# A decoder trunk's prologue rewritten: loads, conditioning row and row scale

## Chip, cores and metric

One core of a Trainium2 chip runs the whole kernel. The metric is device time in microseconds (us) of one execution; lower is better. The engines are TensorE (PE in the rows, PEld where it loads weights), VectorE (DVE), ScalarE (ACT), GpSimd (POOL) and SyncE (SP), which issues the loads.

## What is computed

One layer on 256 tokens of 1024 channels, in float32. Cut to the part that matters here:

```python
shift, scale, gate = jnp.split(c @ w_ada[l] + b_ada[l], 3, axis=-1)
h = rmsnorm(x, norm_pre[l]) * (1.0 + scale[:, None]) + shift[:, None]
proj = h @ w_in[l] + b_in[l]
...
out = merged @ w_out[l]
x = x + gate[:, None] * rmsnorm(out, norm_post[l])
```

`rmsnorm` divides each token's row by the root of its mean square plus 1e-6. Between `proj` and `merged` lie three token mixers, which the change does not touch.

## The kernel before

Python code issues the instructions of all engines in one order, written out by `trunk`; a class `Loom` estimates when each instruction ends and weaves side work between the matrix products. Each engine executes its own instructions strictly in that order. Almost every instruction goes through one helper line, L158, so the rows tell instructions apart by their tiles.

**Prologue (L295 to L460).** TensorE first multiplies a tile of ones with itself (`heat`, L299; `HEAT = (9, 8, 12)` gives the number of products at the three places), so that its clock rises. SP loads the first half of x (128 tokens, `x_sb[:, 0]`), the row c, the second half of x and a few parameters (`p_sb`), in this order (L311 to L314). VectorE clears `c_sb` first (L308), because c fills one row of a 128-row tile, and SP's load of c waits for that. Two products with ones put c into every partition (`ps_cb`, L322); ScalarE copies them to `cb`.

For each half t of the tokens (L441): the sum of squares (ScalarE for t = 0, VectorE for t = 1), then `rsqrt` (L420: reciprocal on VectorE, root on ScalarE, and three small VectorE operations that refine it), then ScalarE multiplies the rows by the result, and eight TensorE transposes (`flip`, tile `ps_x`) turn channels into partitions. A run of `heat` products follows each half. `evac_x` copies the transposed blocks to `xn`: first those of channels 0 to 511 (`evac_x(0, ...)` on ScalarE), the others on VectorE inside the first step of the next loop (L489).

**Wave stage (L475).** Eight steps k, one for each 128 channels. Each loads 1 MB of `w_ada` (`a_raw`) and 1 MB of input weights (`w_raw`); VectorE forms two dot products of `a_raw` with `cb` (`ada_dot`) and from them the columns `acol` and `bcol`; ScalarE splits the weights (`w_hi`) and makes `h_hi` and `h_f` from `xn`, `acol` and `bcol`; VectorE subtracts for the low parts `w_lo` and `h_lo`; TensorE then has 48 products (tile `w`), half of them with the first weight tile, half with the second:

```python
act.copy(hi[0], wraw[:, 0])
if k < CATCH:
    act.copy(hi[1], wraw[:, 1])
act.activation(h_hi[:, k], xn[:, k], AF.Identity, scale=a, bias=b)
act.activation(h, xn[:, k], AF.Identity, scale=a, bias=b)
...
dve.tensor_tensor(lo[0], wraw[:, 0], hi[0], op=OP.subtract)
dve.tensor_tensor(h_lo[:, k], h, h_hi[:, k], op=OP.subtract)
dve.tensor_tensor(lo[1], wraw[:, 1], hi[1], op=OP.subtract)
```

The VectorE dots of step k + 1 stand behind the last of these lines.

**Tail (L1309).** For each half of the tokens two output banks (`ps_out`) are squared on ScalarE with row sums, multiplied by the gate row on VectorE (`weigh`), and after the inverse root multiplied and added to x (`finish`), which also stores them.

Of the kernel before, what the change touches and what calls it, by code (L numbers as in the profile page):

```python
# [18 lines left out]
D = 1024  # L19
# [32 lines left out]

CATCH = 7
AHEAD = {2: ((0, 1), (2,), (3,), ()), 0: ((0,), (1,), (2,), (3,))}
HEAT = (9, 8, 12)
LEAD = 2
BANKS = dict(mm=3, sd=3, ml=2)
BIG, MID = 10, 3
# [6 lines left out]


class Loom:
    """Issues the instructions of every engine in the order of the trace and estimates when each one ends, so that
    side work can be woven between the matrix products once its operands are due."""

    HOP = {"pe": 250.0, "act": 130.0, "dve": 150.0, "dma": 0.0}
    OWN = {"pe": 0.0, "act": 140.0, "dve": 125.0, "dma": 0.0}
# [25 lines left out]
    def drop(self, *tiles):  # L98
        for t in tiles:
            for ring in self.rings.values():  # L100
                if t.tensor.name in ring["live"]:
                    ring["live"].remove(t.tensor.name)
                    ring["free"].append(self.last.get(t.tensor.name, 0.0))
# [37 lines left out]
        return end  # L141

    def clocked(self, start, cost):
        """The tensor engine runs at half its clock after a window in which it was mostly idle."""
        w = int(start // 3413)
        while self.window < w:
            self.cold = self.busy < (0.9 if self.cold else 0.5) * 3413
            self.busy = 0.0
            self.window += 1
        self.busy += cost * (2 if self.cold else 1)  # L150
        return cost * (2 if self.cold else 1)
# [64 lines left out]
                self.tasks.remove(task)  # L216

    def spawn(self, gen, rank=2):
        """Ranks: 0 for what the tensor engine needs next, 1 for the chains of the heads, 2 for the rest."""
        task = [0.0, gen, False, rank]  # L220
        i = next((i for i, t in enumerate(self.tasks) if t[3] > rank or (t[3] == rank == 1)), len(self.tasks))
        self.tasks.insert(i, task)
        return task
# [34 lines left out]
def trunk(ctx: ExitStack, tc, xtok, crow, wada, wave0, wgrp, wmisc, w1, wbr, wout, par, vbias, out):  # L258
# [30 lines left out]
    def mm(o, l, r, start, stop, **kw):  # L289
        return pe.matmul(o, l, r, start=start, stop=stop, **kw)  # L290
# [3 lines left out]

    ones = const.tile([128, 128], F32, name="ones")  # L295
    pool.memset(ones, 1.0)
    warm = const.tile([128, 1], F32, name="warm")

    def heat(n):  # L299
        ps = bank("ps_heat")  # L300
        for _ in range(n):
            mm(ps[:, 0:128], ones, ones, True, True)
        drop(ps)

    heat(HEAT[0])
    act.activation(warm, ones[:, 0:1], AF.Sqrt)
    c_sb = midt("c_sb", [128, D])
    dve.memset(c_sb, 0.0)  # L308
    x_sb = bigt("x_sb", shape=[128, 2, D])
    p_sb = const.tile([128, NPAR], F32, name="p_sb")  # L310
    loom.load(nc.sync, x_sb[:, 0], xtok[:, 0:D])  # L311
    loom.load(nc.sync, c_sb[0:1, :], crow)
    loom.load(nc.sync, x_sb[:, 1], xtok[:, D:2 * D])
    loom.load(nc.sync, p_sb[:, 0:NEARLY], par[:, 0:NEARLY])  # L314

    def pc(name, i=0, n=1):
        return p_sb[:, PAR[name] + i:PAR[name] + i + n]
# [3 lines left out]
    cb = const.tile([128, D], F32, name="cb")  # L321
    ps_cb = [bank("ps_cb", "sd") for _ in range(2)]  # L322
    for i in range(2):
        mm(ps_cb[i], ones, c_sb[:, 512 * i:512 * i + 512], True, True)

    def causal(o, rows_ge_cols, fill):
        pool.affine_select(out=o, in_=o, compare_op=OP.is_ge, fill=fill, base=0,
# [100 lines left out]
    def at_once(gen):  # L428
        for _ in gen:
            pass  # L430
# [5 lines left out]
    def evac_x(i, copy):  # L436
        for t in range(2):
            copy(xn[:, 4 * i:4 * i + 4, 128 * t:128 * t + 128], ptr[t][i].rearrange("p (k q) -> p k q", k=4))
            drop(ptr[t][i])

    for t in range(2):  # L441
        ss, r, n = [work.tile([128, 1], F32, name=f"x{n}{t}", bufs=1) for n in "srn"]
        if t == 0:
            act.activation(xnf[:, 0:D], x_sb[:, 0], AF.Square, accum_out=ss)
        else:
            dve.scalar_tensor_tensor(xnf[:, D:2 * D], x_sb[:, 1], 1.0, x_sb[:, 1], op0=OP.mult, op1=OP.mult,
                                     accum_out=ss)
        dve.tensor_scalar(ss, ss, 1.0 / D, 1e-6, op0=OP.mult, op1=OP.add)
        at_once(rsqrt(ss, r, n))
        for i in range(2):  # L450
            c = x_sb[:, t, 512 * i:512 * i + 512]
            act.activation(c, c, AF.Copy, scale=r)
            for k in range(4):
                flip(ptr[t][i][:, 128 * k:128 * k + 128], c[:, 128 * k:128 * k + 128])
        if t == 0:
            for i in range(2):
                act.copy(cb[:, 512 * i:512 * i + 512], ps_cb[i])
                drop(ps_cb[i])
        heat(HEAT[1 + t])
    evac_x(0, act.copy)  # L460

    adac = const.tile([128, 24], F32, name="adac")

# [11 lines left out]
    for k in range(KT):  # L475
# [833 lines left out]
    for t in range(2):  # L1309
        for fs in (range(tail, KT - 1), range(KT - 1, KT)) if t == 0 else (range(tail, KT),):  # L1310
            for c in range(2):
                for f in fs:
                    out_mm(t, c, f)
        r, v, n = [work.tile([128, 1], F32, name=f"o{x}", tag=f"o{x}") for x in "rvn"]
        ss = [work.tile([128, 1], F32, name=f"ss{c}", tag=f"ss{c}") for c in range(2)]
        rs.append(r)
        res.append(midt("res", [128, 2, 512]))
        for c in range(2):
            scr = work.tile([128, 512], F32, name="sqo", tag="p_t")
            act.activation(scr, po[t][c], AF.Square, accum_out=ss[c])  # L1320
        weigh(t, 0)
        dve.tensor_scalar(ss[0], ss[0], D * 1e-6, None, op0=OP.add)
        if t == 0:
            weigh(t, 1)
        else:
            finish(0, 1)
        dve.tensor_scalar(v, ss[0], ss[1], 1.0 / D, op0=OP.add, op1=OP.mult)
        dve.reciprocal(r, v)
        act.activation(r, r, AF.Sqrt)
        if t == 1:  # L1330
            weigh(t, 1)
        dve.tensor_scalar(n, v, r, r, op0=OP.mult, op1=OP.mult)
        dve.scalar_tensor_tensor(r, n, -3.0, r, op0=OP.add, op1=OP.mult)
        finish(t, 0)
# [89 lines left out]
```

## Time and profile before

| | us |
|---|---|
| median of 3 runs | 512.8 |
| the runs | 513.61, 512.29, 512.80 |
| span of the profiled execution (first to last instruction) | 510.6 |
| TensorE busy in that span | 502.0 (98%) |
| VectorE busy | 431.5 (85%) |
| ScalarE busy | 316.9 (62%) |

Of the profiled execution the span is given, not the time around it; the median of the runs is 2.2 us above that span. A row of the timeline has the start in us from the span's start, the time from the start of its first instruction to the end of its last, engine, line, operation, output<-inputs, shape and count; in brackets, the idle time before and what ended it. Matmul records overlap, so the step from one to the next is shorter than the time of one.

### The profile page before, as it was taken

To read this page: it belongs to the slowest core of one execution; us is meant where nothing else is said; L and a number is where in the kernel's file an instruction comes from. 1 tells how busy PE (TensorE), PEld (TensorE's weight loads), DVE (VectorE), ACT (ScalarE), POOL (GpSimd) and SP (SyncE) were. 2 spreads that over 40 slices of the span, in tenths; PEclk is the share of its full clock that TensorE was granted. 3 is DMA by queue.
4 is the path that set the end of the run, shared out by engine and by line. 5 is a ranking of instruction groups with operands and counts; after the bars stand their busy time and mean duration, and the time that the engine had idled before them with its cause. 6 is when DMAs were issued, how large, how long until landed. Compare 5 with 4: busy or idle time off the path is not lost.

```text
span 510.6 us, 10012 instructions
## 1 busy us (share of the span) xinstructions
PE 502.0 (98%) x3962; PEld 476.6 (93%) x3962; DVE 431.5 (85%) x894; ACT 316.9 (62%) x542; POOL 7.5 (1%) x42
## 2 busy tenths in 40 slices
PE   8999999999999999999999999999999999999994
PEld 6999999899889989979999989999999999999983
DVE  4998888899987998988989968999899997667755
ACT  5556666244566867779568995665534466975442
POOL 4000000000000000000000000000000000000000
PEclk9999999999999999999999999999999999999999
DMA  7999975884694424422523415544675664445502
GB/s 263 380 367 367 421 236 189 292 323 167 223 358 163 164 83 166 143 105 90 190 119 134 162 60 210 197 166 171 243 282 213 235 254 172 166 166 198 214 1 82
DMA packets 17617, 103.86 MB, mean 203 GB/s; under 512 B 2081, under 2 KB 2209, under 8 KB 7458
## 3 DMA queue, kind: packets, MB, share of 16 engines
q1 hardware_dynamic: 17570, 103.22, 55.0%
q8 instruction: 31, 0.51, 0.4%
q14 instruction: 16, 0.13, 0.1%
HBM read 102.16 MB, written 1.05 MB: 202 GB/s over the span
## 4 chain that ended last, share of the span: by engine, by line
PE 96%; DMA 1%; DVE 1%; ACT 0%; issue 0%; DVEq 0%; SPq 0%; ACTq 0%
PE ps_f L158 50%; PE ps_br L158 14%; PE w L158 9%; PE ps_t L158 7%; PE ps_out L158 4%; PE ps_o L158 3%; PE ps_s L158 2%; PE ps_c L158 2%; PE ps_p L158 1%; DMA x_sb<-in_xtok_dram 1%; PE ps_n L158 1%; PE ps_qk L158 1%; PE ps_heat L158 1%; PE ps_g L158 0%; PE ps_ht L158 0%; PE ps_mb L158 0%
## 5 line engine op out<-in xcount | busy, mean ns | idle before, releaser
L158 DVE TENSOR_TENSOR w_lo<-w_raw,w_hi 128x1024 fp32r<-128x1024 f32 x148 | 180.3, 1221 | 34.5 <-ACT w_hi L158 34.2
L158 ACT CAST w_hi<-w_raw 128x1024 fp32r<-128x1024 f32 x148 | 154.1, 1043 | 57.1 <-PE ps_br L158 16.9
L158 PE MATMUL ps_f<-h_hi,w_hi 128*128 128x256 f32 x704 | 177.4, 288 | 0.0
L158 PE MATMUL ps_f<-h_lo,w_hi 128*128 128x256 f32 x704 | 173.5, 283 | 0.0
L158 PEld LDWEIGHTS ps_f<-h_hi,w_hi 128*128 128x128 f32 x704 | 134.8, 192 | 2.2 <-issue 1.9
L158 PEld LDWEIGHTS ps_f<-h_lo,w_hi 128*128 128x128 f32 x704 | 134.9, 192 | 0.6 <-issue 0.2
L158 PE MATMUL ps_f<-h_hi,w_lo 128*128 128x256 f32 x704 | 102.7, 287 | 0.0
L158 DVE SCALAR_TENSOR_TENSOR acc<-u,p_sb,acc 128x226 f32<-128x226 f32 (+28 forms) x232 | 94.5, 463 | 8.6 <-ACT acc L158 8.4
L158 PEld LDWEIGHTS ps_f<-h_hi,w_lo 128*128 128x128 f32 x704 | 91.5, 192 | 2.4 <-issue 2.3
L158 ACT ACT_TABLE_LOAD x27 | 34.6, 1283 | 1.3 <-PEq L1416 0.8
L158 PE MATMUL w<-h_lo,w_hi 128*128 128x256 f32 x128 | 31.4, 283 | 0.0
L158 PE MATMUL w<-h_hi,w_lo 128*128 128x256 f32 x128 | 31.4, 283 | 0.0
L158 PE MATMUL ps_t<-w_hi,h_hi 128*128 128x256 f32 x96 | 29.6, 308 | 0.0
L158 DVE SCALAR_TENSOR_TENSOR a_raw<-a_raw,cb 128x1024 f32<-128x1024 f32 x24 | 28.5, 1220 | 0.0
L158 PE MATMUL ps_t<-w_hi,h_lo 128*128 128x256 f32 x96 | 27.1, 283 | 0.0
L158 PE MATMUL ps_t<-w_lo,h_hi 128*128 128x256 f32 x96 | 27.1, 282 | 0.0
L158 PEld LDWEIGHTS w<-h_hi,w_lo 128*128 128x128 f32 x128 | 24.6, 192 | 0.0
L158 PEld LDWEIGHTS w<-h_lo,w_hi 128*128 128x128 f32 x128 | 24.6, 192 | 0.0
L158 ACT ACTIVATE gs<-ps_f,p_sb 128x256 f32<-128x256 f32 x16 | 7.6, 476 | 25.5 <-PE ps_f L158 22.7
L158 PEld LDWEIGHTS ps_t<-w_hi,h_hi 128*128 128x128 f32 x96 | 18.3, 191 | 2.0 <-issue 1.7
L158 ACT ACTIVATE pm<-pm,mx 128x16 f32<-128x16 f32 (+2 forms) x48 | 19.1, 403 | 0.8 <-DVE mx L158 0.8
L158 PEld LDWEIGHTS ps_t<-w_lo,h_hi 128*128 128x128 f32 x96 | 18.3, 191 | 0.7 <-issue 0.5
(268 smaller groups left out, 777.0 us busy)
## 6 DMA issues: line engine op xcount, KB each, us to landing
w_raw<-in_wgrp_dram SPq DMA_DIRECT2D x50, 1024.0 KB, 4.9
w_raw<-in_wbr_dram SPq DMA_DIRECT2D x12, 1024.0 KB, 4.8
a_raw<-in_wada_dram SPq DMA_DIRECT2D x16, 512.0 KB, 7.3
w_raw<-in_wave_dram SPq DMA_DIRECT2D x16, 512.0 KB, 7.3
w_raw<-in_w_dram SPq DMA_DIRECT2D x8, 1024.0 KB, 4.9
a_raw<-in_wada_dram SPq DMA_DIRECT2D x4, 1024.0 KB, 5.2
w_raw<-in_wout_dram SPq DMA_DIRECT2D x4, 1024.0 KB, 4.9
x_sb<-in_xtok_dram SPq DMA_DIRECT2D x2, 512.0 KB, 4.7
```

What stands on the lines that cost most here:

```text
L158: inst = self.pin(fn(*args, **kw))
```

## The change

- c goes to ScalarE's load queue, and the parameters behind it; both halves of x stand alone at the head of SP's queue. The clearing of `c_sb` is gone: the products that spread c use one row of ones and one row of c. VectorE, not ScalarE, copies them to `cb`, at the head of its order.
- The row scale is no longer multiplied into x. It is put on the diagonal of a 128x128 tile (`diag`, VectorE), and eight float32 products of x with that tile transpose and scale at once; they take the place of the transposes.
- Both sums of squares are on ScalarE, and the root is taken straight from them (a tile `eps` holds 1e-6); VectorE then inverts and refines once.
- `HEAT` is (9, 6, 6).
- In step k = 0 of the wave stage ScalarE copies the other blocks of `xn` behind `h_f`, and the second weight tile's `w_hi` behind them; VectorE's copies of `xn` are gone.
- The tail takes the root straight from the sums too, and the order of `weigh` and the small operations on VectorE changes.

```diff
-HEAT = (9, 8, 12)
+HEAT = (9, 6, 6)
...
+    loom.load(nc.scalar, c_sb[0:1, :], crow)
+    for t in range(2):
+        loom.load(nc.sync, x_sb[:, t], xtok[:, D * t:D * t + D])
+    loom.load(nc.scalar, p_sb[:, 0:NEARLY], par[:, 0:NEARLY])
     heat(HEAT[0])
     act.activation(warm, ones[:, 0:1], AF.Sqrt)
-    dve.memset(c_sb, 0.0)
-    loom.load(nc.sync, x_sb[:, 0], xtok[:, 0:D])
-    loom.load(nc.sync, c_sb[0:1, :], crow)
-    loom.load(nc.sync, x_sb[:, 1], xtok[:, D:2 * D])
-    loom.load(nc.sync, p_sb[:, 0:NEARLY], par[:, 0:NEARLY])
...
-        mm(ps_cb[i], ones, c_sb[:, 512 * i:512 * i + 512], True, True)
+        mm(ps_cb[i], ones[0:1, :], c_sb[0:1, 512 * i:512 * i + 512], True, True)
+        dve.tensor_copy(cb[:, 512 * i:512 * i + 512], ps_cb[i])
+        drop(ps_cb[i])
...
+        act.activation(xnf[:, D * t:D * t + D], x_sb[:, t], AF.Square, accum_out=ss)
+        act.activation(r, ss, AF.Sqrt, bias=eps, scale=1.0 / D)
...
+        dve.tensor_scalar(v, ss, 1.0 / D, 1e-6, op0=OP.mult, op1=OP.add)
+        dve.reciprocal(r, r)
+        dve.tensor_scalar(n, v, r, r, op0=OP.mult, op1=OP.mult)
+        dve.scalar_tensor_tensor(r, n, -3.0, r, op0=OP.add, op1=OP.mult)
+        dve.tensor_scalar(diag, ident, r, -0.5, op0=OP.mult, op1=OP.mult)
         for i in range(2):
-            c = x_sb[:, t, 512 * i:512 * i + 512]
-            act.activation(c, c, AF.Copy, scale=r)
             for k in range(4):
-                flip(ptr[t][i][:, 128 * k:128 * k + 128], c[:, 128 * k:128 * k + 128])
+                mm(ptr[t][i][:, 128 * k:128 * k + 128], x_sb[:, t, 512 * i + 128 * k:512 * i + 128 * k + 128], diag,
+                   True, True)
         heat(HEAT[1 + t])
...
-        if k == 0:
-            evac_x(1, dve.tensor_copy)
...
-        if k < CATCH:
+        if 0 < k < CATCH:
             act.copy(hi[1], wraw[:, 1])
         act.activation(h_hi[:, k], xn[:, k], AF.Identity, scale=a, bias=b)
         act.activation(h, xn[:, k], AF.Identity, scale=a, bias=b)
-        if k >= CATCH:
+        if k == 0:
+            for t in range(2):
+                evac_x(t, 1)
+        if k == 0 or k >= CATCH:
             act.copy(hi[1], wraw[:, 1])
...
+        act.activation(r, ss[1], AF.Sqrt, bias=ss[0], scale=1.0 / D)
...
-        dve.reciprocal(r, v)
-        act.activation(r, r, AF.Sqrt)
...
+        dve.reciprocal(r, r)
```

In the built programs the orders of the engines differ in the prologue, in the first step of the wave stage and in the tail, and nowhere between. VectorE in the prologue, before (`xs` are the sums of squares, `xr` and `xn_...` the scale and its refinement, `a_raw,adac` the first dots):

```order
L158 SCALAR_TENSOR_TENSOR xn,xs_184<-x_sb 128x1024
L158 TENSOR_SCALAR xs_184<-xs_184 128x1
L158 RECIPROCAL xr_185<-xs_184 128x1
L158 TENSOR_TENSOR xn_186<-xr_185,xs_184 128x1
L158 SCALAR_TENSOR_TENSOR xn_186<-xn_186,xr_185 128x1
L158 SCALAR_TENSOR_TENSOR xr_185<-xn_186,xr_185 128x1
L158 SCALAR_TENSOR_TENSOR a_raw,adac<-a_raw,cb 128x1024 x2
```

VectorE at the same place in the changed program:

```order
L158 COPY cb<-ps_cb 128x512 x2
L158 TENSOR_SCALAR xv_159<-xs_156 128x1
L158 RECIPROCAL xr_157<-xr_157 128x1
L158 TENSOR_SCALAR xn_158<-xv_159,xr_157 128x1
L158 SCALAR_TENSOR_TENSOR xr_157<-xn_158,xr_157 128x1
L158 TENSOR_SCALAR diag_168<-ident,xr_157 128x128
L158 TENSOR_SCALAR xv_165<-xs_162 128x1
L158 RECIPROCAL xr_163<-xr_163 128x1
L158 TENSOR_SCALAR xn_164<-xv_165,xr_163 128x1
L158 SCALAR_TENSOR_TENSOR xr_163<-xn_164,xr_163 128x1
L158 TENSOR_SCALAR diag_189<-ident,xr_163 128x128
L158 SCALAR_TENSOR_TENSOR a_raw,adac<-a_raw,cb 128x1024 x2
```

The copies of `ps_cb` now stand ahead of both scale chains. TensorE from its start to the first product of the wave stage, before:

```order
L158 MATMUL ps_heat<-ones 128x128 x9
L158 MATMUL ps_cb<-c_sb,ones 128x512 x2
L158 MATMUL ps_x<-ident,x_sb 128x128 x8
L158 MATMUL ps_heat<-ones 128x128 x8
L158 MATMUL ps_x<-ident,x_sb 128x128 x8
L158 MATMUL ps_heat<-ones 128x128 x12
L158 MATMUL w_0_225<-h_hi,w_hi 128x256 x2
```

TensorE, changed:

```order
L158 MATMUL ps_heat<-ones 128x128 x9
L158 MATMUL ps_cb<-c_sb,ones 128x512 x2
L158 MATMUL ps_x<-diag_168,x_sb 128x128 x8
L158 MATMUL ps_heat<-ones 128x128 x6
L158 MATMUL ps_x<-diag_189,x_sb 128x128 x8
L158 MATMUL ps_heat<-ones 128x128 x6
L158 MATMUL w_0_218<-h_hi,w_hi 128x256 x2
```

The places are the same; transposes became products, and there are eight `heat` products fewer. ScalarE from the first copy of `xn` to the `h_hi` of step k = 1, before:

```order
L158 COPY xn<-ps_x 128x4x128 x2
L158 CAST w_hi<-w_raw 128x1024 x2
L158 ACTIVATE h_hi<-xn,bcol,acol 128x256
L158 ACTIVATE h_f<-xn,bcol,acol 128x256
L158 CAST w_hi<-w_raw 128x1024 x2
L158 ACTIVATE h_hi<-xn,bcol,acol 128x256
```

ScalarE, changed:

```order
L158 COPY xn<-ps_x 128x4x128 x2
L158 CAST w_hi<-w_raw 128x1024
L158 ACTIVATE h_hi<-xn,bcol,acol 128x256
L158 ACTIVATE h_f<-xn,bcol,acol 128x256
L158 COPY xn<-ps_x 128x4x128 x2
L158 CAST w_hi<-w_raw 128x1024 x3
L158 ACTIVATE h_hi<-xn,bcol,acol 128x256
```

The second `w_hi` of step 0 moved from ahead of `h_hi` to behind two more copies.

## Rows read from the trace of the kernel before

**Rows 1.** The page's chain that ended last, shares by engine.
```profile
PE 96%; DMA 1%; DVE 1%; ACT 0%; issue 0%; DVEq 0%; SPq 0%; ACTq 0%
```
**Rows 2.** That chain in order of time: start us, us, what.
```profile
1.08 0.92 DVE c_sb L158
...
2.38 5.78 DMA x_sb<-in_xtok_dram
...
12.70 2.68 PE ps_heat L158 x24
15.39 46.33 PE w L158 x384
```
**Rows 3.** All that TensorE waited for: us in total, times, longest.
```profile
PE ps_heat L158 <- POOL ones L296: 1.1, 1, 1.1
PE ps_x L158 <- ACT x_sb L158: 0.7, 1, 0.7
```
**Rows 4.** Timeline of SP's queue: the first load.
```profile
0.80 0.38 SPq L187 DMA_DIRECT2D x_sb<-in_xtok_dram  x1
```
**Rows 5.** TensorE in the prologue: two tile views (ns min/median/max), two timeline rows.
```profile
L158 PE MATMUL ps_heat<-ones x17: 421/421/582, 1.1 to 4.6; 128*128 128x128 f32 x17
L158 PE MATMUL ps_heat<-ones x16: 275/275/275, 8.8 to 10.4; 128*128 128x128 f32 x16
5.06 2.97 PE L158 MATMUL ps_cb<-c_sb,ones 128*128 128x512 f32 x4
7.86 1.05 PE L158 MATMUL ps_x<-ident,x_sb 128*128 128x128 f32 x8
```
**Rows 6.** Timeline of VectorE, 9.4 to 20 us.
```profile
9.45 0.15 DVE L158 TENSOR_SCALAR xs<-xs 128x1 f32<-128x1 f32 x1
9.64 0.16 DVE L158 RECIPROCAL xr<-xs 128x1 f32<-128x1 f32 x1
...
10.53 1.22 DVE L158 SCALAR_TENSOR_TENSOR a_raw<-a_raw,cb 128x1024 f32<-128x1024 f32 x1
...
13.09 1.28 DVE L158 COPY xn<-ps_x 128x512 f32<-128x512 f32 x2
...
16.20 1.22 DVE L158 TENSOR_TENSOR w_lo<-w_raw,w_hi 128x1024 fp32r<-128x1024 f32 x1
17.34 1.22 DVE L158 SCALAR_TENSOR_TENSOR a_raw<-a_raw,cb 128x1024 f32<-128x1024 f32 x1
...
19.82 0.16 DVE L158 TENSOR_TENSOR acol<-acol,p_sb 128x1 f32<-128x1 f32 x1
```
**Rows 7.** Timeline of ScalarE, 11.9 to 20.6 us.
```profile
11.89 1.05 ACT L158 COPY xn<-ps_x 128x512 f32<-128x512 f32 x2
12.84 2.00 ACT L158 CAST w_hi<-w_raw 128x1024 fp32r<-128x1024 f32 x2
14.73 0.60 ACT L158 ACTIVATE h_hi<-xn,bcol,acol 128x256 fp32r<-128x256 f32 x1
15.23 0.59 ACT L158 ACTIVATE h_f<-xn,bcol,acol 128x256 f32<-128x256 f32 x1
...
20.02 0.60 ACT L158 ACTIVATE h_hi<-xn,bcol,acol 128x256 fp32r<-128x256 f32 x1
```
**Rows 8.** Timeline: TensorE's first weight load of step k = 1.
```profile
21.12 1.03 PEld L158 LDWEIGHTS w<-h_hi,w_hi 128*128 128x128 f32 x8
```
**Rows 9.** Timeline of VectorE at the end.
```profile
504.57 0.21 DVE L158 TENSOR_SCALAR ov<-ss,ss 128x1 f32<-128x1 f32 x1 [0.28 <-ACT sqo L158]
...
504.89 0.67 DVE L158 TENSOR_TENSOR res<-ps_out,gprow 128x512 f32<-128x512 f32 x1
505.48 0.27 DVE L158 TENSOR_SCALAR on<-ov,or 128x1 f32<-128x1 f32 x1
```
**Rows 10.** Windows at the end: us, busy by engine, granted clock (PEclk), DMA.
```profile
505.60:509.00 3.40, 0.00 (x0) 0.00 (x0) 1.72 (x4) 0.00 (x0) 0.00 (x0) 1.00 0.47 180
509.00:510.60 1.60, 0.00 (x0) 0.00 (x0) 0.00 (x0) 0.00 (x0) 0.00 (x0) 0.50 0.00 0
```

More of the change, by code (lines that the diff above doesn't have):

```diff
@@ L296, in trunk @@
     pool.memset(ones, 1.0)
+    eps = const.tile([128, 1], F32, name="eps")
+    pool.memset(eps, 1e-6)
     warm = const.tile([128, 1], F32, name="warm")
@@ L303, in heat @@
         drop(ps)
+    c_sb = midt("c_sb", [128, D])
+    x_sb = bigt("x_sb", shape=[128, 2, D])
+    p_sb = const.tile([128, NPAR], F32, name="p_sb")
+    loom.load(nc.scalar, c_sb[0:1, :], crow)
+    for t in range(2):
+        loom.load(nc.sync, x_sb[:, t], xtok[:, D * t:D * t + D])
+    loom.load(nc.scalar, p_sb[:, 0:NEARLY], par[:, 0:NEARLY])
     heat(HEAT[0])
     act.activation(warm, ones[:, 0:1], AF.Sqrt)
-    c_sb = midt("c_sb", [128, D])
-    dve.memset(c_sb, 0.0)
-    x_sb = bigt("x_sb", shape=[128, 2, D])
-    p_sb = const.tile([128, NPAR], F32, name="p_sb")
-    loom.load(nc.sync, x_sb[:, 0], xtok[:, 0:D])
-    loom.load(nc.sync, c_sb[0:1, :], crow)
-    loom.load(nc.sync, x_sb[:, 1], xtok[:, D:2 * D])
-    loom.load(nc.sync, p_sb[:, 0:NEARLY], par[:, 0:NEARLY])
     def pc(name, i=0, n=1):
@@ L434, in trunk, with evac_x @@
     ptr = [[bank("ps_x", "ml" if t == 0 else "sd") for i in range(2)] for t in range(2)]
[L436 to L439, printed above, removed]
+    def evac_x(t, i):
+        act.copy(xn[:, 4 * i:4 * i + 4, 128 * t:128 * t + 128], ptr[t][i].rearrange("p (k q) -> p k q", k=4))
+        drop(ptr[t][i])
+    scales = []
     for t in range(2):
[L442 to L449, printed above, removed]
+        ss, r, n, v = [work.tile([128, 1], F32, name=f"x{n}{t}", bufs=1) for n in "srnv"]
+        act.activation(xnf[:, D * t:D * t + D], x_sb[:, t], AF.Square, accum_out=ss)
+        act.activation(r, ss, AF.Sqrt, bias=eps, scale=1.0 / D)
+        scales.append((ss, r, n, v))
+    for t in range(2):
+        ss, r, n, v = scales[t]
+        diag = const.tile([128, 128], F32, name=f"diag{t}")
+        dve.tensor_scalar(v, ss, 1.0 / D, 1e-6, op0=OP.mult, op1=OP.add)
[3 more added lines that the diff above has]
+        dve.tensor_scalar(diag, ident, r, -0.5, op0=OP.mult, op1=OP.mult)
         for i in range(2):
-            c = x_sb[:, t, 512 * i:512 * i + 512]
-            act.activation(c, c, AF.Copy, scale=r)
             for k in range(4):
-                flip(ptr[t][i][:, 128 * k:128 * k + 128], c[:, 128 * k:128 * k + 128])
[L455 to L458, printed above, removed]
+                mm(ptr[t][i][:, 128 * k:128 * k + 128], x_sb[:, t, 512 * i + 128 * k:512 * i + 128 * k + 128], diag,
+                   True, True)
         heat(HEAT[1 + t])
-    evac_x(0, act.copy)
+    for t in range(2):
+        evac_x(t, 0)
     adac = const.tile([128, 24], F32, name="adac")
@@ L497, in trunk @@
         act.activation(h, xn[:, k], AF.Identity, scale=a, bias=b)
-        if k >= CATCH:
+        if k == 0:
+            for t in range(2):
+                evac_x(t, 1)
+        if k == 0 or k >= CATCH:
             act.copy(hi[1], wraw[:, 1])
@@ L1320, in trunk @@
             act.activation(scr, po[t][c], AF.Square, accum_out=ss[c])
+            if c == 0:
+                dve.tensor_scalar(ss[0], ss[0], 1.0 / D, 1e-6, op0=OP.mult, op1=OP.add)
+        act.activation(r, ss[1], AF.Sqrt, bias=ss[0], scale=1.0 / D)
         weigh(t, 0)
-        dve.tensor_scalar(ss[0], ss[0], D * 1e-6, None, op0=OP.add)
         if t == 0:
@@ L1326, in trunk @@
             finish(0, 1)
-        dve.tensor_scalar(v, ss[0], ss[1], 1.0 / D, op0=OP.add, op1=OP.mult)
-        dve.reciprocal(r, v)
-        act.activation(r, r, AF.Sqrt)
-        if t == 1:
             weigh(t, 1)
+        dve.tensor_scalar(v, ss[1], 1.0 / D, ss[0], op0=OP.mult, op1=OP.add)
+        dve.reciprocal(r, r)
         dve.tensor_scalar(n, v, r, r, op0=OP.mult, op1=OP.mult)
```

## Prediction

> **What bounds the kernel.** I read the chain that ended last first: 96% of it is TensorE [rows 1]. In order of time it says where that begins. A clearing on VectorE, the load of x's second half (5.78 us) and the work behind it end in `heat` products, and from 15.39 on the chain is TensorE alone [rows 2]. The list of TensorE's waits confirms it: two waits in the whole span, both in the prologue [rows 3]. So three numbers decide about this change: S, the moment at which the wave stage's first product starts (15.39); any stall that TensorE gets behind S; and the chain behind its last product. Whatever happens to other engines costs nothing unless it moves one of these three, and what moves them moves the end by as much.
>
> **S, step by step.** The loads drop out first. SP's first load starts at 0.80 [rows 4], the second can now follow in its place some 0.4 later instead of at 2.38; if it takes the old 5.78 us [rows 2] it lands at 7.0, c much sooner. Neither is what S waits for, as follows.
>
> TensorE starts with nine `heat` products as before. Each float32 product is two passes (17 records stand for some eight products); the steps between passes are 0.22 there, (4.6-1.1)/16, and 0.11 later, (10.4-8.8)/15 [rows 5]: the lower and the upper of the clock's two levels, 1.2 and 2.4 GHz. The two products that spread c run between, from 5.06 to 8.03 [rows 5]. They now have one row instead of 128, and no row shows what that saves: from below nothing would be left of the 2.97, from above all. I take all, for the cost of a pass follows the columns: 512 columns take about four times the 0.22 of 128 at the same level. On the Trainium skill's page "TensorE: Matmul & The Clock Gate", section on what happens when a matmul is issued, the time of the weight load goes with the columns and not the rows, too.
>
> Then the new link. VectorE's order begins with two copies of these products, so both scale chains, ready since about 6, wait for TensorE to finish at 8.03. One copy from PSUM takes a step of about 0.64 (1.28 for two [rows 6]); the first runs under the second product, the second ends the wait at 8.03 + 0.05 + 0.6 = 8.68. The scale chain follows: three dependent small steps at 0.19 (9.45 to 9.64 [rows 6]), one with two column operands that takes 0.27 [rows 9] plus 0.04, and the diagonal tile. That operation is not in the trace; it lies between 0.15 (one column [rows 6]) and 0.64 (512 columns); I take 0.30, since 128 columns are nearer the lower end. The tile is there at about 9.85.
>
> TensorE: eight products instead of eight transposes. Eight transposes took 1.05 with their drain, one pass each [rows 5]; a product is two passes, so 8 x 2 x 0.112 = 1.79. Six `heat` products take 1.34. First half 9.85 to 11.64, `heat` to 12.98, the second half's first four products to 13.88, and 0.16 more until they are through (a record of 275 ns against a step of 112 [rows 5]): 14.04. The second `heat` ends at 12.98 + 1.79 + 1.34 = 16.11. So `heat` between the halves is no longer cover: the second tile is ready at about 10.8, and its products queue behind it.
>
> ScalarE copies that block (start 14.09), then needs a step of 0.475 (two copies 11.89 to 12.84), 0.945 for one `w_hi` (two from 12.84 to 14.73) and 0.60 for `h_hi` [rows 7]: 14.09 + 0.475 + 0.945 + 0.60 = 16.11. S = 16.14, against 15.39: **+0.75**. The conditioning columns are no later than before: VectorE starts the dots at about 10.5 in both (10.53 [rows 6]). The sum of squares that moved to ScalarE (about 1.3 with its root) fits between the landing at 7 and 9.9, when VectorE asks for it; it costs nothing, and up to 2 us of lateness of that load stays hidden too.
>
> **A stall at step k = 1: +1.10.** Before, VectorE's last operation of step 0 started at 16.20; from there to the end of the next `h_hi` (20.02 + 0.60 = 20.62 [rows 6, 7]) are 4.42 us: that subtraction, two dots, three small operations, `h_hi`. TensorE needed it at 21.12 [rows 8], 5.73 after S, so 0.5 was spare. Now that subtraction waits for the second `w_hi`, which on ScalarE stands behind `h_f` and two copies: `h_hi` starts at S - 0.63, `h_f` 0.50 later [rows 7], the copies 0.50 after that, the `w_hi` 0.95 after them, and ends 1.05 later, at S + 2.37. The subtraction starts at S + 2.41, and `h_hi` of k = 1 is there at S + 6.83. TensorE is through with step 0 at S + 5.73: it waits 1.10. That VectorE is rid of two copies (1.28 [rows 6]) doesn't help, since it is waiting for ScalarE in that time. In steps 2 to 7 the orders are the old ones, and VectorE's work of a step is shorter than TensorE's 5.73; the wait is neither repeated nor won back, because TensorE has no other idle time in which to win it [rows 3].
>
> **The tail: 0.** The root now starts without VectorE's step, but the chain gains nothing: VectorE's last `weigh`, which waits for the same square as `ov` at 504.57 did, moves ahead of it, takes a step of 0.59 (504.89 to 505.48 [rows 9]) and then scale, inverse and refinement follow: 504.57 + 0.59 + 0.10 + 0.19 = 505.45, where `on` stood at 505.48. I put bounds of -0.1 and +0.1.
>
> **The sum, and the clock.** +0.75 + 1.10 + 0 = +1.85 against the profiled execution. One term in it is a matter of the moment at which TensorE's clock rises: the c products are now on the path, and this trace shows them partly at the lower level. All at the upper level they would take half of 4 x 0.85 = 3.4, 1.7 plus drain, and end at 6.9 (S earlier by 1.1, +0.75 in the sum); all at the lower level they would end at 8.6 (+2.45). The trace lies near the late end of these bounds, so I take half a microsecond off: **+1.35**. On the page named above, section "The HAM clock gate", that moment shifts by about half a microsecond from run to run; by it alone the sum would be 1.85 give or take 0.25, the median 514.65. The median of the runs is 512.8, 2.2 above the span of the profiled execution; with the part around the span unchanged I predict 512.8 + 1.3 = **514.1**.
>
> **Rivals.**
> 1. *The clock falls in the new gap, or rises late (slower).* Between the c products' last pass and the first diagonal product TensorE idles some 1.8 us (8.0 to 9.85), which it didn't before. If the lower level came back there, the 6.26 us of passes between 9.85 and S would run at half rate until the clock rose again; the start of the program shows about 6 us of passes before the upper level (1.1 to between 5 and 8 [rows 5]), half of them lost: +3.1, so 517.2. If it falls late in the gap or lasts half as long, 515.7. Decisive is whether 1.8 us idle are enough. Against it: after the last product TensorE was idle for 3.4 us at a granted clock of 1.00, and only then did a window show 0.50 [rows 10]. The same page, section "HAM oscillation", says that idle stretches between bursts put the clock back and each burst then starts slow; the rows above bound how long it takes here.
> 2. *The clock is up when the c products start.* Then the sum is +0.75 less what the earlier second `heat` saves: 513.4. For it: nothing in this trace, where the passes at 5.06 are slow; it needs a different moment of the rise.
> 3. *No stall.* If TensorE's step 1 doesn't wait (VectorE's dots hidden after all), +0.25 to +0.75: 513.3. Against it: the strict orders shown ahead.
> 4. *The load of x was the bound after all (faster).* It stands in the chain with 5.78 us behind 0.92 of clearing [rows 2]. If S follows it, 1.2 us are won at S, some more by a shorter chain, and without the stall 511.2 results. Against it: it needs the c products off the path, and they stand ahead of the scale in VectorE's order.
>
> **Chances.** The sum as worked out, with the clock's moment and the diagonal tile uncertain, 0.62 (513.3 to 515.2); rival 1 0.14; rivals 2 and 3 0.19; rival 4 0.05. 0.3% is 1.5 us, about what a measurement of this kernel can tell from no change; 514.1 is 0.25% above the median, so the main case falls on both sides of the bound, slower beyond it in four of ten. Slower: 0.62 x 0.42 + 0.14 = 0.40. Faster by over 0.3%: 0.04. Same: 0.56. The range of 8 in 10 reaches from rivals 2 and 3 to the milder form of rival 1: 512.8 to 515.9.
>
> **What would show it.** In the changed profile: `cb` copied by VectorE at about 8.1 to 8.7 and the diagonal tile right behind; S at 15.0 to 16.7; TensorE waiting about 1.1 us for `h_hi` between the 48th and 49th wave product, and nowhere later; second half of x landed before 8. The forecast is wrong if S is below 15, if the step from first to second wave step stays at 5.7, or if passes of 0.22 stand behind the gap.

## The result and the profile after

| | before | changed |
|---|---|---|
| median, us | 512.71 (4 runs, 512.29 to 513.61) | 517.02 (4 runs, 515.82 to 518.90) |
| ratio | | 1.0087, 95% interval 1.0066 to 1.0109 |
| span of the profiled execution | 510.6 | 516.3 |
| wave stage starts (S) | 15.39 | 20.04 |
| from S to the first weight load of the second wave step | 5.73 | 6.84 |

The kernel became slower by 0.9%, and 517.0 lies above the range. The spans of the two profiled executions differ by 5.7 us, the medians by 4.3: the profiled execution of the changed kernel took 518.01, one us more than its median. The list of all that TensorE waited for in the changed kernel answers to [rows 3]:

```profile
PE ps_x L158 <- DVE xv L158: 1.8, 1, 1.8
PE ps_heat L158 <- POOL eps L298: 1.1, 1, 1.1
PE w L158 <- ACT h_hi L158: 0.7, 1, 0.7
```

All three are waits that the prediction had counted; the 1.8 and the 0.7 are the new ones. So what was lost beyond the forecast is not waiting. The timeline of TensorE in the changed prologue (columns as in [rows 4]):

```profile
5.19 3.78 PE L158 MATMUL ps_cb<-c_sb,ones 1*128 1x512 f32 x4
10.78 3.78 PE L158 MATMUL ps_x<-diag,x_sb 128*128 128x128 f32 x16 [1.82 <-DVE xv L158]
14.36 2.66 PE L158 MATMUL ps_heat<-ones 128*128 128x128 f32 x12
16.86 1.95 PE L158 MATMUL ps_x<-diag,x_sb 128*128 128x128 f32 x16
18.65 1.50 PE L158 MATMUL ps_heat<-ones 128*128 128x128 f32 x12
20.04 1.21 PE L158 MATMUL w<-h_hi,w_hi 128*128 128x256 f32 x8
```

The same work stands here twice, at two speeds. Sixteen passes of diagonal products step from 10.78 to 14.36, 0.22 each; the next sixteen from 16.86 to 18.65, 0.11 each. The twelve heat passes between them step at 0.21. So TensorE was at the lower level (1.2 GHz) until about 16.8; before the change the level rose at about 7.2, inside the c products: their four passes took 2.80 there [rows 5], which is 2.6 of them at 0.85, as the slow ones of this profile, and the others at half of that. The PEclk column shows 1.00 throughout this prologue, while the passes step at 0.21: ahead of the first change on record it tells nothing, and the level has to be read from the step of the passes.

VectorE in between, timeline of the changed kernel:

```profile
7.30 0.69 DVE L158 COPY cb<-ps_cb 128x512 f32<-128x512 f32 x1 [7.30 <-PE ps_cb L158]
9.01 0.69 DVE L158 COPY cb<-ps_cb 128x512 f32<-128x512 f32 x1 [1.01 <-PE ps_cb L158]
9.61 0.14 DVE L158 TENSOR_SCALAR xv<-xs 128x1 f32<-128x1 f32 x1
...
10.44 0.29 DVE L158 TENSOR_SCALAR diag<-ident,xr 128x128 f32<-128x128 f32 x1
```

The link is the forecast one: the copies wait for TensorE's c products, and the first diagonal tile comes behind them. At the second wave step (timeline, VectorE's last subtraction of the first step and its next dot, then TensorE's first weight load of the second):

```profile
22.41 1.23 DVE L158 TENSOR_TENSOR w_lo<-w_raw,w_hi 128x1024 fp32r<-128x1024 f32 x1 [1.33 <-ACT w_hi L158]
23.56 1.22 DVE L158 SCALAR_TENSOR_TENSOR a_raw<-a_raw,cb 128x1024 f32<-128x1024 f32 x1
26.88 0.53 PEld L158 LDWEIGHTS w<-h_hi,w_hi 128*128 128x128 f32 x4 [0.90 <-ACT h_hi L158]
```

The subtraction starts at S + 2.37, the second step at S + 6.84 where it used to be S + 5.73 [rows 8]. The waits view gives 0.7 for it and this row 0.90, since each counts from the end of the work ahead on its own queue (products, weight loads), and the ends of products are modelled; the distance of the starts gives 1.11. At the end, `on` stands at

```profile
511.16 0.27 DVE L158 TENSOR_SCALAR on<-ov,or 128x1 f32<-128x1 f32 x1
```

5.68 later than before [rows 9], against 4.65 (20.04 - 15.39) + 1.11 = 5.76 by S and the second step: nothing else of weight was won or lost, the tail gave 0.08.

### The profile page after: what moved, and what is told of

It reads as the page before. It is cut to its first block, busy times and chain, and to the rows that moved or that the text cites. A ratio compares the mean times of both kernels' runs of the same rounds, so it can differ in the third digit from the quotient of the medians.

```text
span 516.3 us, 10006 instructions
## 1 busy us (share of the span) xinstructions
PE 505.9 (98%) x3962; PEld 479.6 (93%) x3962; DVE 429.8 (83%) x891; ACT 316.1 (61%) x540; POOL 7.5 (1%) x43
## 3 DMA queue, kind: packets, MB, share of 16 engines
HBM read 102.16 MB, written 1.05 MB: 200 GB/s over the span
## 4 chain that ended last, share of the span: by engine, by line
PE 96%; DVE 2%; ACT 1%; issue 0%; DVEq 0%; POOL 0%; POOLq 0%
PE ps_f L158 49%; PE ps_br L158 13%; PE w L158 8%; PE ps_t L158 7%; PE ps_out L158 4%; PE ps_o L158 3%; PE ps_s L158 2%; PE ps_c L158 2%; PE ps_p L158 1%; PE ps_heat L158 1%; PE ps_n L158 1%; PE ps_qk L158 1%; PE ps_x L158 1%; PE ps_cb L158 1%; DVE a_raw L158 0%; ACT w_hi L158 0%
```

## The experiments

Two theories compete for the late rise of the clock. **Rows**: a product with one row doesn't do for the clock what one with 128 rows does. **Gap**: the 1.8 us without work ahead of the diagonal products put it back. A third, **moment**, is that the rise only wanders. Each experiment has its own runs of the kernel before beside it (medians 512.2 to 512.7), and its ratio is against these.

### 128 rows in the changed kernel, first try

```diff
+    dve.memset(c_sb, 0.0)
     loom.load(nc.scalar, c_sb[0:1, :], crow)
...
-        mm(ps_cb[i], ones[0:1, :], c_sb[0:1, 512 * i:512 * i + 512], True, True)
+        mm(ps_cb[i], ones, c_sb[:, 512 * i:512 * i + 512], True, True)
```

> The changed kernel, with the two products that spread c over all 128 rows again (VectorE clears the tile first, ScalarE's load of c waits for that). In the changed kernel TensorE's passes went from 0.213 to 0.112 us at 16.8 us from the start, before the change at 7.2. Theory 'rows': products with one row do not bring TensorE's clock up, those with 128 do. Then the passes get fast within the c products again, at about 7.2; these end at 8.0 instead of 9.0, the diagonal products and the first heat run at 0.112 (2.6 us less), the wave stage starts at about 16.4 instead of 20.0, and the median is about 513.4. Rival 'gap': the 1.8 us in which TensorE waits for the first diagonal tile set the clock back. The gap is still there, so the wave stage starts at 19 to 20 and the median stays at 516 to 517.

Measured: 516.92 (ratio 1.0100, 1.0080 to 1.0119). That looks like "gap", but the edit made a second gap. One line of TensorE's waits, and windows (us, busy by engine, granted clock, DMA):

```profile
PE ps_cb L158 <- DMA c_sb<-in_crow_dram: 2.2, 1, 2.2
```

```profile
4.00:5.00 1.00, 0.79 (x6) 0.59 (x5) 0.00 (x0) 0.62 (x3) 1.00 (x9) 1.00 1.02 410
...
6.00:7.00 1.00, 0.04 (x1) 0.07 (x1) 0.00 (x0) 0.94 (x2) 0.99 (x4) 1.00 0.99 337
7.00:8.00 1.00, 1.00 (x2) 0.47 (x3) 0.00 (x0) 0.69 (x3) 0.00 (x0) 0.78 1.00 385
8.00:9.00 1.00, 1.00 (x2) 0.34 (x1) 0.54 (x1) 0.00 (x0) 0.00 (x0) 0.50 1.02 405
...
17.00:18.00 1.00, 1.00 (x8) 1.00 (x7) 0.00 (x0) 0.00 (x0) 0.00 (x0) 0.60 0.86 266
```

c, loaded behind the clearing, landed at 7.0. TensorE idled from 4.8 to 7.0, and the clock fell at about 7.55 (0.78 is the mean of 1.00 for 0.56 us and 0.50 for the rest). The trace shows a fall behind an idle stretch of 2.2 us, 2.8 after its start; of the rows it tells nothing, and the fifth run repairs that. It does show something of the gap: with the clock low, 128-row products stood on both sides of the 1.8 us, which are idle here too, and the clock rose only at about 17.8 (0.60 is the mean of 0.50 for 0.8 us and 1.00 for the rest), 5.8 us after the first diagonal product.

### One row in the kernel before

```diff
-        mm(ps_cb[i], ones, c_sb[:, 512 * i:512 * i + 512], True, True)
+        mm(ps_cb[i], ones[0:1, :], c_sb[0:1, 512 * i:512 * i + 512], True, True)
```

> The kernel before, with one edit: the two products that spread c multiply one row of ones with one row of c (the tile is still cleared, all loads and orders are the old ones). Theory 'rows': the clock does not rise in these products any more; they end at 8.8 instead of 8.0, the transposes and most of the 40 heat passes behind them run at 0.213 instead of 0.112, the wave stage starts 1.5 to 4 us later (17 to 19.5), median 514.2 to 516.7. Rival 'gap' and rival 'moment' (the rise only wanders from run to run): nothing changes but what the products save, 512.0 to 512.8.

Measured: 514.66 (ratio 1.0050, 1.0038 to 1.0062). TensorE's only wait in the whole span is the one at its start; its timeline:

```profile
PE ps_heat L158 <- POOL ones L296: 1.1, 1, 1.1
```

```profile
5.19 3.78 PE L158 MATMUL ps_cb<-c_sb,ones 1*128 1x512 f32 x4
8.90 1.97 PE L158 MATMUL ps_x<-ident,x_sb 128*128 128x128 f32 x8
10.66 3.25 PE L158 MATMUL ps_heat<-ones 128*128 128x128 f32 x16
13.75 1.04 PE L158 MATMUL ps_x<-ident,x_sb 128*128 128x128 f32 x8
...
17.41 0.39 PE L158 MATMUL w<-h_hi,w_hi 128*128 128x256 f32 x1
```

The eight transposes take 0.22 each at 8.90 and 0.11 at 13.75. Of the 16 heat passes, 3.09 us from 10.66 to 13.75, some 13 are slow: the clock rose at about 13.4 instead of 7.2, though TensorE never idled once it had started, and S is 17.41 instead of 15.39. The one row saves no time in the products themselves: 5.19 to 8.90 is four passes of 0.93, where 128 rows had 0.70 with the rise inside [rows 5]. This shows "rows" as a cause that works without any gap. What the gap adds to it in the changed kernel, whose clock rose another 3.4 us later, the run doesn't tell. On the Trainium skill's page "TensorE: Matmul & The Clock Gate", section "The HAM clock gate", the rise goes by time of activity and not by the number of products, and rows are not mentioned; taken by itself, that gives no reason for a later rise here, where TensorE is busy without a break. The measurement decides: one row did make the rise later.

### Heat in the gap of the changed kernel

```diff
         drop(ps_cb[i])
+    heat(4)
```

> The changed kernel, with four more heat products directly behind the two c products, which fill the 1.8 us in which TensorE waited for the first diagonal tile. Theory 'gap': with no idle stretch the clock rises before the diagonal products or early in them, the wave stage starts at about 16.5 to 17.5 and the median is 513.3 to 514.5. Theory 'rows': the work of 128 rows begins anew at 9.0 instead of 10.8, and the rise comes 1.8 us earlier at most, at about 15; of the 28 slow passes some 17 earlier ones stay slow, the wave stage starts at about 19.2, median 516 to 516.5.

Measured: 514.80 (ratio 1.0053, 1.0041 to 1.0065), between the two. Timeline of TensorE, then windows:

```profile
5.19 2.00 PE L158 MATMUL ps_cb<-c_sb,ones 1*128 1x512 f32 x4
7.12 1.16 PE L158 MATMUL ps_heat<-ones 128*128 128x128 f32 x8
9.01 3.51 PE L158 MATMUL ps_x<-diag,x_sb 128*128 128x128 f32 x16 [0.73 <-DVE xv L158]
```

```profile
7.00:8.00 1.00, 1.00 (x8) 0.88 (x8) 0.83 (x4) 0.69 (x3) 0.00 (x0) 1.00 1.02 418
8.00:9.00 1.00, 0.28 (x3) 0.09 (x1) 0.81 (x6) 0.00 (x0) 0.00 (x0) 0.84 1.02 410
9.00:10.00 1.00, 0.99 (x4) 0.99 (x5) 0.89 (x6) 0.00 (x0) 0.00 (x0) 0.50 1.05 426
```

In this execution the clock was up when the one-row products ran (2.00 us, not 3.78) and fell at about 8.7, after an idle stretch of only 0.4. What TensorE did before was two us of one-row products and eight heat passes. Neither theory had foreseen this form. All five executions lie within 0.7 us and show the same mean granted clock, 0.994, so they seem to have taken this course. Whether the one-row products or the idle stretch lowered the clock, this run does not separate; that longer stretches behind products with 128 rows did not lower it (below) speaks for the products.

### The old order of the first wave step

```diff
-        if 0 < k < CATCH:
+        if k < CATCH:
             act.copy(hi[1], wraw[:, 1])
...
-        if k == 0:
-            for t in range(2):
-                evac_x(t, 1)
-        if k == 0 or k >= CATCH:
+        if k >= CATCH:
```

VectorE copies `evac_x(t, 1)` ahead of that, as before the change.

> The changed kernel, with the old order of the wave stage's first step: ScalarE makes both w_hi ahead of h_hi, VectorE copies the second half of xn. In the changed kernel TensorE waited 0.7 us between the first and the second step. Theory 'order': that wait goes (step 0.0 to 0.1), but h_hi of step 0 ends one w_hi later (0.95) unless the first heat after the clock's rise hides it; the wave stage's start moves from 20.04 to about 20.4 (h_hi was ready at 19.98, heat ended at 20.0), so the sum is -0.7 +0.9, median 516.9 to 517.3, the same. Rival: the wait has another cause (VectorE's two dots follow at the same distance) and stays at 0.7; then the median is 517.9.

Measured: 515.99 (ratio 1.0067, 1.0054 to 1.0080). TensorE's first weight load of the second step, and then the only wait listed behind the diagonal products:

```profile
25.21 0.43 PEld L158 LDWEIGHTS w<-h_hi,w_hi 128*128 128x128 f32 x3
```

```profile
PE w L158 <- ACT h_hi L158: 0.8, 1, 0.8
```

S is 19.48, so the second step follows after 5.73, as in the kernel before, without a wait. The 0.8 stand at S itself, since `h_hi` now ends one `w_hi` later. So the order explains the wait at the second step, as forecast; by this trace it gains only what the later `h_hi` leaves, 1.11 - 0.83 = 0.28. The median lies below both expectations, and S was not the expected 20.4, because in this execution the clock rose at about 13.6, some 3 us earlier than in the changed kernel's profile, with the same prologue up to there. So the moment does wander between executions. The times of the changed kernel scatter by 3.1 us in four runs, those of the kernel before by 2.0 in the 29 that stand beside the next run, which fits.

### 128 rows in the changed kernel, c in time

```diff
-    loom.load(nc.scalar, c_sb[0:1, :], crow)
-    for t in range(2):
-        loom.load(nc.sync, x_sb[:, t], xtok[:, D * t:D * t + D])
+    dve.memset(c_sb, 0.0)
+    loom.load(nc.sync, x_sb[:, 0], xtok[:, 0:D])
+    loom.load(nc.sync, c_sb[0:1, :], crow)
+    loom.load(nc.sync, x_sb[:, 1], xtok[:, D:2 * D])
```

and the products of 128 rows as in the first try.

> The changed kernel with 128-row c products, as in the first of these experiments, but c is loaded where the kernel before loads it (on SP's queue between the halves of x), so that it is there when the first heat ends and no new idle stretch comes ahead of the c products. Left is the idle stretch of 1.8 us ahead of the first diagonal product. Theory 'rows': the clock rises in the c products (they end at 8.0 to 8.6), the diagonal products run at 0.112, the wave stage starts at 16.2 to 17.2, median 513.0 to 514.0 (1.1 of it the wait at the second step). Rival 'gap': the idle stretch alone puts the clock back or keeps it low; the diagonal products run at 0.213, the wave stage starts at 19 or later, median 516 or more.

Measured: 513.73 (ratio 1.0021, 1.0011 to 1.0032), against 1.0087 for the changed kernel. TensorE's timeline:

```profile
5.30 2.60 PE L158 MATMUL ps_cb<-c_sb,ones 128*128 128x512 f32 x4
9.72 2.05 PE L158 MATMUL ps_x<-diag,x_sb 128*128 128x128 f32 x16 [1.82 <-DVE xv L158]
11.61 1.50 PE L158 MATMUL ps_heat<-ones 128*128 128x128 f32 x12
12.95 1.95 PE L158 MATMUL ps_x<-diag,x_sb 128*128 128x128 f32 x16
...
16.12 1.22 PE L158 MATMUL w<-h_hi,w_hi 128*128 128x256 f32 x8
```

The idle stretch of 1.82 is still there, and behind it all passes step at 0.11: behind products with 128 rows, which brought the clock up, this stretch did not lower it. None of the eleven executions shows a lower mean granted clock (0.995 to 0.999) than the kernel before beside them (0.995 to 0.998). So the gap alone does not cost the 3.9 us, and the rows do make the difference, as in "One row in the kernel before", where they were the only edit (here c's load moves too). It does not follow that the gap is harmless where the clock is still low: in the first try it rose 5.8 us behind the stretch.

S is 16.12, where the prediction's working had 16.14, and the span is 512.4: 1.8 above that of before, the prediction's +1.85. In part this is luck: the c products end 0.13 earlier than in the working (7.90, not 8.03), and the way from the first diagonal product to S is 0.11 longer (6.40, not 6.29).

### The scale chains ahead of the copies of c

VectorE's two copies of `ps_cb` move behind both scale chains; the products keep one row.

```diff
-        dve.tensor_copy(cb[:, 512 * i:512 * i + 512], ps_cb[i])
-        drop(ps_cb[i])
...
         heat(HEAT[1 + t])
+    for i in range(2):
+        dve.tensor_copy(cb[:, 512 * i:512 * i + 512], ps_cb[i])
+        drop(ps_cb[i])
```

> The changed kernel, with VectorE's two copies of the c products behind both scale chains instead of ahead of them. The first diagonal tile is then ready at about 7.5, while TensorE is still in its one-row c products (to 9.0), so that the idle stretch of 1.8 us goes and only the one-row products are left. Theory 'rows': the case is the same as the kernel before with one-row products, which never idled and whose clock rose at 13.4: the diagonal products run slow from 9.0 to 12.4, the wave stage starts at 17.2 to 18.5, median 514.5 to 516. Rival 'gap': without the stretch the clock is up by 9.0, the wave stage starts at 15.4 to 16, median 512.2 to 512.9.

Measured: 513.48 (ratio 1.0019, 1.0005 to 1.0033), between the two expectations, with twelve times in three groups: three at 511.9 to 512.3, six at 513.4 to 513.6, three at 515.2 to 515.4. The middle group has a mean granted clock of 0.992 to 0.995, the others 0.997 or 0.998. The profiled execution shows why one number was too simple. TensorE's one short wait, and windows:

```profile
7.44 2.93 PE L158 MATMUL ps_x<-diag,x_sb 128*128 128x128 f32 x16 [0.34 <-DVE diag L158]
```

```profile
6.00:7.00 1.00, 1.00 (x3) 0.18 (x1) 0.68 (x4) 1.00 (x2) 1.00 (x4) 1.00 1.01 390
7.00:8.00 1.00, 0.66 (x6) 0.56 (x6) 0.69 (x4) 0.62 (x3) 0.00 (x0) 1.00 1.00 410
8.00:9.00 1.00, 1.00 (x9) 1.00 (x8) 0.93 (x4) 0.29 (x1) 0.00 (x0) 0.70 1.05 414
9.00:10.00 1.00, 1.00 (x7) 1.00 (x7) 0.96 (x3) 0.29 (x1) 0.00 (x0) 0.50 1.00 410
```

The profile is one of the middle group. The clock, up since 5.0 here, fell at about 8.4 in the middle of the diagonal products, with 0.34 us idle before them and two us of one-row products before that. The executions of this one kernel lie up to 3.5 us apart; the granted clocks of the groups fit a clock that is up early and stays, one that falls as here, and one that rises late, but the other two have no trace.

### c spread by its load, and that once more

No c products: `cb` is loaded into all partitions behind x (512 KB), 16 heat products stand ahead of the diagonal ones, none between, 10 behind.

```diff
-HEAT = (9, 6, 6)
+HEAT = (16, 0, 10)
...
+    loom.load(nc.sync, cb, crow.broadcast_to([128, D]))
...
-        mm(ps_cb[i], ones[0:1, :], c_sb[0:1, 512 * i:512 * i + 512], True, True)
-        dve.tensor_copy(cb[:, 512 * i:512 * i + 512], ps_cb[i])
```

The products and copies of `ps_cb` are gone. In the first wave step VectorE copies `evac_x(t, 1)`, ScalarE's second `w_hi` stays behind `h_f`.

> The changed kernel without the c products: one load spreads c into all partitions of cb (512 KB on SP's queue behind x). TensorE runs 128-row heat from its start to the first diagonal tile (16 products), no heat between the halves and 10 after them; VectorE copies the second half of xn, as before the change, the second w_hi of the first step stays behind h_f. If one-row products and the waits on them are what cost, then the clock is up by 5 to 8 and stays up, the diagonal products start at 7.5 to 8.2 at 0.112, the wave stage starts at 13.3 to 14 (w_hi and h_hi of the second half's first block end last), the wait at the second step is 0.3 to 0.6, median 510.2 to 511.2: faster than both. Rival: the extra 512 KB make the weights of the first step late (they land 1.3 us later), the wave stage starts at 15 or later, median 512 or more; or the clock falls without c products too, then 514.

Measured: 512.52 (ratio 0.9993, 0.9985 to 1.0002): no change that can be told, short of the 510.2 to 511.2 expected. The profiled execution took 511.3, the other ten 512.45 to 512.69. For the trace of one near 512.5, the same kernel once more:

> The kernel that loads c into all partitions, once more for its trace: ten of its eleven executions took 512.5, the profiled one 511.3. Should this one be near 512.5, its trace says where the 1.2 us lie. Theory 'landing': the loads of the first step's weights land later and the wave stage starts at about 14.9. Theory 'clock': the clock rises or falls at another moment, and passes of 0.213 stand behind 7.8. Theory 'second step': the wave stage starts at 13.7 and TensorE waits more than 1 us at the second step.

It took 512.52. Both traces start the wave stage at 13.7 with the clock up. At the second step, ScalarE's second `w_hi` in the first and in the second of these runs:

```profile
18.56 1.05 ACT L158 CAST w_hi<-w_raw 128x1024 fp32r<-128x1024 f32 x1 [0.29 <-DMA w_raw<-in_wave_dram]
```

```profile
19.75 1.05 ACT L158 CAST w_hi<-w_raw 128x1024 fp32r<-128x1024 f32 x1 [1.50 <-DMA w_raw<-in_wave_dram]
```

The start of 13.7 was right. Of the 1.7 us won there the first run keeps 1.0 at the second step (weight load at 20.16, against 21.12 before), and the second run gives all of it back (21.34): its weights land 1.2 later ("second step"). Why they do stays open. The extra 512 KB stand in front of them in both runs, and no run here takes them away alone.

### c spread through the identity

c is loaded as 128 rows of 8; VectorE multiplies them with the identity into a 128x1024 tile, and ones times that tile gives `cb`, with 128 rows and nothing to clear.

```diff
+    loom.load(nc.scalar, c8, crow.rearrange("o (p j) -> (o p) j", j=8))
...
+    dve.tensor_tensor(c_sb.rearrange("p (q j) -> p q j", j=8), ident.unsqueeze(2).to_broadcast([128, 128, 8]),
+                      c8.unsqueeze(1).to_broadcast([128, 128, 8]), op=OP.mult)
...
+        mm(ps_cb[i], ones, c_sb[:, 512 * i:512 * i + 512], True, True)
...
-        dve.tensor_copy(cb[:, 512 * i:512 * i + 512], ps_cb[i])
+        act.copy(cb[:, 512 * i:512 * i + 512], ps_cb[i])
```

`HEAT` is (9, 0, 6). ScalarE's copies of `ps_cb` leave VectorE free for the scale chains. In the first wave step ScalarE copies `evac_x(1, 0)` behind the first `w_hi`, its second `w_hi` comes ahead of `evac_x(t, 1)`, and VectorE takes the first dot of step two, whose `a_raw` is loaded earlier for it, ahead of its last subtraction.

> The changed kernel with c products of 128 rows that need neither a cleared tile nor a longer load: c is loaded as 128 rows of 8, VectorE multiplies it with the identity into a 128x1024 tile, ones times that tile gives cb. ScalarE copies cb, the scale chains come first on VectorE, no heat between the halves. In the first step of the wave stage ScalarE makes the second w_hi ahead of its last copies of xn, and VectorE takes the first dot of the second step ahead of the last subtraction. Theory 'rows': the clock is up by 5 to 8.5, diagonal products run at 0.112 from 7.6 to 8.3, the wave stage starts at 12.7 to 13.4, TensorE's wait at the second step is 0 to 0.4, span 507.9 to 509.0, median 509.8 to 511.0, faster than both. Rival: the start of the wave stage is tied to the weights' landing and to VectorE's dots and gains nothing below 13.7, or a wait at the second step takes it back: median 511.5 or more.

Measured: 511.14 (ratio 0.9970, 0.9957 to 0.9983): faster than both kernels, but above the expected 509.8 to 511.0. Several edits act together here; no run separates them. TensorE's timeline:

```profile
6.39 3.78 PE L158 MATMUL ps_cb<-c_sb,ones 128*128 128x512 f32 x4 [1.14 <-DVE c_sb L158]
9.97 3.87 PE L158 MATMUL ps_x<-diag,x_sb 128*128 128x128 f32 x32
...
14.94 0.36 PE L158 MATMUL w<-h_hi,w_hi 128*128 128x256 f32 x1
```

There is no wait at the second step any more. But c landed only at 5.1, TensorE idled 1.14 and the clock rose at about 10.2, so S was 14.94, not 13. Here the c products have 128 rows and run at the lower level; they take 3.78, to the hundredth what those with one row took in the changed kernel. Three more heat products are to fill the idle stretch:

```diff
-HEAT = (9, 0, 6)
+HEAT = (12, 0, 6)
```

> The kernel before this one (c spread through the identity) with twelve heat products at the start instead of nine. There TensorE stood idle from 5.3 to 6.4, because c landed at 5.1, and the clock rose at 10.2, so that the c products took 3.4 us instead of 1.7. Theory 'rows': with 128-row work up to 6.3 the clock is up at 7.6 at the latest, the c products end at 8.2 to 8.9, the wave stage starts at 13.2 to 14.0 with no wait at the second step, median 509.5 to 510.6. Rival: the landing of the weights and the dots hold the start at 14.9 whatever the clock does, or the rise is as late as before: median 511.0 or more.

Measured: **510.40** (ratio 0.9959, 0.9946 to 0.9973), the lowest median here, though its interval overlaps that of the run before. The profiled execution is the slowest of the five (511.56, the others 510.1 to 510.6). Timeline of TensorE, then its longest wait:

```profile
6.43 1.98 PE L158 MATMUL ps_cb<-c_sb,ones 128*128 128x512 f32 x4 [1.08 <-DVE c_sb L158]
...
13.08 0.72 PE L158 MATMUL w<-h_hi,w_hi 128*128 128x256 f32 x4
```

```profile
PE w L158 <- ACT h_hi L158: 1.4, 1, 1.4
```

In this execution the clock rose so early (3.9) that the heat products ended by 5.34 and the idle stretch remained; it did not lower the clock. S is 13.08. The median lies within the forecast; that it came there in the forecast way this trace does not show, since the clock was up before the three added products ran. What limits this execution next is the wait of 1.4 at the third step, where ScalarE waits for the weights' landing; whether the four others had it, no trace shows.

## Why the prediction was wrong

**Where the argument stood.** That S, a stall behind it and the tail decide, and nothing else, held in the profiled execution: 4.65 + 1.11 - 0.08 = 5.68, within 0.02 of the difference of the spans.

**The loads drop out, the new link, the diagonal tile.** Right. From the end of the c products to the first diagonal product were forecast 9.85 - 8.03 = 1.82 and measured 10.78 - 8.97 = 1.81.

**The stall at the second step.** Right: 1.10 forecast, 1.11 measured, and the old order takes it away.

**The tail.** Right: within the bounds of 0.1.

**The sum, and the clock.** This is the step that failed. It let the one-row products cost what columns cost, which was right, and asked only when within them the clock would rise; the moment was bounded by 6.9 and 8.6 for their end, and half a us was taken off. That the clock might not rise in them at all, so that the passes behind them run at the lower level too, was not in the bounds; the half us was taken off in the wrong direction. They ended at 8.97, 0.94 behind the working and 0.37 behind its late bound, and from the first diagonal product to S passed 20.04 - 10.78 = 9.26 instead of 16.14 - 9.85 = 6.29: 28 passes, 16 diagonal and 12 of heat, at 0.21 instead of 0.11, which is 2.8 of these 2.97. Together 3.9, the whole distance between 16.14 and 20.04. With 128 rows, and c loaded as before the change, the kernel starts the wave stage at 16.12. The prediction had named its own sign for this: passes of 0.22 behind the gap.

How much of the 3.9 the gap has a part in stays open. With the one-row products and no gap the clock rose at 13.4, in the changed kernel at 16.8 and 13.6. With the one-row products kept, heat in the gap brought the ratio from 1.0087 to 1.0053, and the scale chains ahead of the copies, which also shorten the path, to 1.0019.

**The first rival** named 517.2 for a clock that falls in the gap or rises late. That 517.02 lies so near is luck: it is the middle of two executions at 515.8 and 516.0 and two at 518.0 and 518.9. In the profiled one "rises late" came true, and not for the rival's reason: the clock was not up ahead of the gap, so nothing could fall in it, and with 128 rows the same stretch did not lower it. The two shorter executions have no trace, but a mean granted clock of 0.989. Of 514 us that is some 11 us at the lower level on record, where the profiled one has 4.6, at its end; if their ends are alike, an estimate from these figures is that the clock in these two had risen and then fallen again for some 6 to 7 us. Whether it fell in the gap is not shown. The rival had 0.14, because the rows at the end of the trace, 3.4 us idle ahead of a fall, spoke against a fall in 1.8. Falls came sooner here (2.8 us after the idle stretch began in the first experiment, 0.4 in the third), and no row was asked about what the products ahead of the gap do. The rule quoted from the Trainium skill's page "TensorE: Matmul & The Clock Gate", section "HAM oscillation", that idle stretches put the clock back, is borne out by the 2.2 us of the first experiment and not by the 1.8 behind 128-row products in the fifth.

**Rivals 2 to 4.** The clock was not up when the c products started in the changed kernel's profile, the stall came, and S did not follow x's load, which had landed ahead of its square at 6.23 (the working said 7.0).

## What to carry to other kernels

Don't cut the rows of products that stand ahead of the clock's rise to save time: here products with one row took as long as those with 128 (2.00 and 1.98 us for the two at the upper level, 3.78 for both at the lower), and in three traces in which the clock was not up when they began, it rose only 4 to 8 us behind them, with every pass until then at half the speed. Numbers of rows between 1 and 128 were not measured. When an edit changes the shape of products in the first microseconds, compare the step of the passes behind them, not the waits: the lost 3.9 us stand in no list of waits. An order that lets VectorE wait for a late ScalarE result is priced well by adding up the chain to the next `h_hi`, here within 0.01 us at the second step.

## What was not expected of the hardware

A clock that is up can fall behind one-row products. In two profiled executions it was up when they ran and fell at about 8.7 and 8.4, after 2 us of them and idle stretches of 0.4 and 0.34, while 1.82, 1.37 and 1.08 us of idle time behind products with 128 rows did not lower it in three others. (The 1.37 stand ahead of the diagonal products in the second run with c spread by its load.)

And the moment of the rise moves by far more than the half microsecond with which the prediction reckoned. TensorE starts at 1.05 in every trace, and in eight of the twelve the clock rose before the 128-row products that come first had ended, at 3.9, 4.1, 4.2, 5.0, 5.3, 6.4, 6.6 and 7.2. In the five traces with one-row products the heat products ahead of them end at about 5.3, and what follows goes with this moment: in the two in which the clock was up by then, it fell behind the one-row products; in the three in which it was not (the changed kernel, one row in the kernel before, the old order), it rose only at 16.8, 13.4 and 13.6.
